# Projections by seven block products, with their results kept in DRAM

## The chip, the cores and the metric

The kernel runs on one core of a Trainium2 chip. The metric is the device time of one execution in microseconds. TensorE multiplies matrices, VectorE and ScalarE do element-wise work, GpSimd (POOL) and SyncE (SP) issue DMA transfers here; the engines run side by side and wait for each other by semaphores.

## The reference

One layer of a decoder trunk on 1024 tokens of 1024 channels, in float32:

```python
h = rms_norm(x, norm_w) * (1.0 + scale) + shift          # shift, scale, gate = silu(c) @ ada_w + ada_b
hq, hf, hi, hz, gq, gk, gv, gz, ga, mg = split(h @ w_in)  # 9232 columns
y_h = hgrn2_branch(hq, hf, hi, hz, ...)   # 8 heads: gated linear recurrence, norm over all, times silu(hz)
y_g = gla_branch(gq, gk, gv, gz, ga, ...) # 4 heads, value width 256, norm per head, times silu(gz)
merged = sigmoid(mg[0]) * (y_h @ w_branch[0]) + sigmoid(mg[1]) * (y_g @ w_branch[1])
out = rms_norm(x + gate * (merged @ w_out), final_norm_w)
```

Both branches are `chunked_gated_linear_attention`: within a chunk all pairs of steps with their decay, between chunks a state of keys by values.

## The kernel before

Every dense product is made of three float32r products: each operand is split into hi + lo (`split`, L150 to L159: a ScalarE copy, L155, and a VectorE subtraction, L158), and hi·hi, hi·lo and lo·hi are summed in PSUM. A `Feat` job makes one tile of 128 features by 1024 tokens: for each of eight k tiles 3 x 2 matmuls of 128x512 (L414). A `Vblk` job makes 256 features of v with tokens on the partitions (L473 to L475, 256 columns a matmul). The jobs run in one list: GLA's projections, the gates of branch 1, branch 1 (`w_branch[0, 1]`), HGRN's projections, the gates of branch 0, branch 0, and the output projection (`OutBlk`, L1078 to L1080). The first six feature tiles are made earlier, k by k, while the modulation is loaded (L309, and L332 for the second half of the tokens).

`Stream.go` runs the jobs; one unit is a k step of six matmuls. `weave` runs a step of the attention when the units that its last `yield` asked for have passed. `ahead` loads weights two jobs ahead and splits them one ahead, if buffers are free. All data stays in SBUF, in 46 buffers of 4 KB per partition (`Slots`); buffers are handed out in program order, first freed first. Only the gated product of branch 1 passes through DRAM (`t1_dram`).

The attention of a head (`attention`, L487 to L663): products of q and decays on VectorE (L504 to L507), small TensorE products of 32 steps (L511, L543, L572, L579, L585) whose results are masked into `blk` and `scT`, scalings of q and k in between (L513 to L549, L591, L592), then transposes of k (L621), state updates (L640, L646) and outputs (L657, L659), which `post` squares and multiplies with the gate.

The order of instructions on each engine comes from a planner that may move ready work ahead of older work; at the start (L124 to L284) the order is that of the program. The engines themselves run their queues in order.

Of the kernel before, what the change touches and what calls it, by code (L numbers as in the profile page):

```python
# [25 lines left out]
N_SLOTS = 46  # L26
ROOM = 9
LOOK = 6


class Slots:
    """Buffers of 4 KB per partition, handed out and given back in program order."""

    def __init__(self, pool, n):
        self.pool = pool
        self.free_list = deque(range(n))
        self.owner = {}
        self.serial = 0

    def get(self, shape, dtype=F32):  # L40
        i = self.free_list.popleft()
        self.serial += 1
        t = self.pool.tile([P] + list(shape), dtype, tag=f"s{i}", name=f"b{self.serial}")
        self.owner[id(t)] = (i, t)
        return t

    def free(self, *tiles):
        for t in tiles:
            self.free_list.append(self.owner.pop(id(t))[0])


@with_exitstack
def hybrid_trunk_kernel(
# [11 lines left out]
    sp = ctx.enter_context(tc.tile_pool(name="slots", bufs=1))  # L65
    dp = ctx.enter_context(tc.tile_pool(name="dram", bufs=1, space=bass.MemoryType.DRAM))
    ps_d = ctx.enter_context(tc.tile_pool(name="ps_d", bufs=2, space=bass.MemoryType.PSUM))
    ps_s = ctx.enter_context(tc.tile_pool(name="ps_s", bufs=1, space=bass.MemoryType.PSUM))
    ps_m = ctx.enter_context(tc.tile_pool(name="ps_m", bufs=2, space=bass.MemoryType.PSUM))
    S = Slots(sp, N_SLOTS)  # L70
    cnt = [0]

    def dtile():
        cnt[0] += 1
        return ps_d.tile([P, T], F32, tag="d", name=f"pd{cnt[0]}")
# [5 lines left out]
    sc_ps = ps_s.tile([P, T], F32, name="sc_ps")  # L81

    # ---------------------------------------------------------------- constants
# [5 lines left out]
    nc.gpsimd.memset(eps_t, EPS)  # L89
    one_t = ones[:, 0:1]  # L90
# [5 lines left out]
    rows_c = cp.tile([8, P], F32, name="rows_c")  # L96
    rows_a = cp.tile([24, P], F32, name="rows_a")
    rows_b = cp.tile([22, P], F32, name="rows_b")
# [5 lines left out]
    def load_x(t):  # L104
        b = S.get([D])
        nc.sync.dma_start(b, x2[t * P:(t + 1) * P, :])
        return b

    row_load(nc.sync, rows_c, c[0])
    x_t = [load_x(t) for t in range(4)]  # L110
# [5 lines left out]
    row_load(nc.gpsimd, rows_b[20:22, :], gla_norm_w[0])  # L116

    def vec_rows(rows, n, at):
        pv = mtile()
        i = nc.tensor.transpose(pv[:, 0:n], rows, ident[0:n, 0:n])  # L120
        nc.vector.tensor_copy(vec[:, at:at + n], pv[:, 0:n])
        return i

    order = ExitStack()  # L124
    order.enter_context(tc.manual_schedule(engines={
        mybir.EngineType.PE, mybir.EngineType.Activation, mybir.EngineType.DVE}))
# [3 lines left out]
    warm = cp.tile([P, 1], F32, name="warm")  # L130
    nc.scalar.activation(warm, cs[:, 0:1], AF.Sqrt)
    nc.vector.tensor_mul(cs, cs, vec[:, R_C:R_C + 8])

    # ---- buffers of the attention, which the start borrows
    scT = cp.tile([P, NCH, P], F32, name="scT")
    blk = cp.tile([P, NCH, 32], F32, name="blk")
    xb = cp.tile([P, 32, 80], F32, name="xb")
    scT_f = scT.rearrange("p c t -> p (c t)")
    xb_f = xb.rearrange("p b c -> p (b c)")

    # ---------------------------------------------------------------- x: norm and transpose, modulation
    h_hi = [S.get([T], F32R) for _ in range(KT)]
    h_lo = [S.get([T], F32R) for _ in range(KT)]
    hT = {}
# [5 lines left out]
    def split(src, hi=None, lo=None, eng=None, pin=False):  # L150
        """src (fp32) = hi + lo with both parts float32r."""
        if hi is None:
            hi = S.get(list(src.shape[1:]), F32R)
            lo = S.get(list(src.shape[1:]), F32R)
        i = nc.scalar.copy(hi, src)  # L155
        if pin:
            tc.keep_in_program_order(i)
        (eng or nc.vector).tensor_sub(lo, src, hi.bitcast(F32))  # L158
        return hi, lo  # L159

    def norm_x(half, xs):
        for i, xt in enumerate(xs):
            t = half * 4 + i
            acc, r = ssx[:, t:t + 1], rsx[:, t:t + 1]
            junk = S.get([D])
            nc.scalar.activation(junk, xt, AF.Square, accum_out=acc)
            S.free(junk)
# [4 lines left out]
    def transpose_x(half, xs, d):  # L172
        if d % 2 == 0:
            hT[half, d // 2] = S.get([2, 512])
        pt = mtile()
        for i in range(4):
            nc.tensor.transpose(pt[:, i * P:(i + 1) * P], xs[i][:, d * P:(d + 1) * P], ident)
        dst = hT[half, d // 2][:, d % 2, :]
        nc.scalar.copy(dst, pt)
        if d == KT - 1:  # L180
            S.free(*xs)

    def make_h(half, d):
        b = hT[half, d // 2][:, d % 2, :]
        sl = slice(half * 512, half * 512 + 512)
        nc.scalar.activation(b, b, AF.Identity, bias=modv[:, 0, d:d + 1], scale=amul[:, d:d + 1])
        split(b, h_hi[d][:, sl], h_lo[d][:, sl])

    def load_mod(d0, nd):
        kq = 4 // nd  # L190
        parts = []
        for kk in range(KT // kq):
            b = S.get([kq, 2, nd * P])
            for half in range(2):
                c0 = half * D + d0 * P
                nc.sync.dma_start(b[:, :, half, :], ada_w[0, kk * kq * P:(kk + 1) * kq * P, c0:c0 + nd * P].rearrange(
                    "(k p) f -> p k f", p=P))
            parts.append(b)
        return parts

    def make_mod(d0, nd, parts, on_pe):
        kq = 4 // nd
        acc = scT_f[:, (d0 // 2 % 2) * 512:(d0 // 2 % 2) * 512 + 2 * nd * P].rearrange("p (a f) -> p a f", a=2)
        for k in range(on_pe, KT):
            src = parts[k // kq][:, k % kq]
            if k == on_pe:
                i = nc.vector.tensor_scalar_mul(acc, src, cs[:, k:k + 1])
                if on_pe:
                    tc.keep_in_program_order(i)
            else:  # L210
                nc.vector.scalar_tensor_tensor(acc, src, cs[:, k:k + 1], acc, ALU.mult, ALU.add)
        pm = mtile()
        for half in range(2):
            for i in range(nd):
                o = pm[:, half * nd + i:half * nd + i + 1]
                for k in range(on_pe):
                    nc.tensor.matmul(o, parts[k // kq][:, k % kq, half, i * P:(i + 1) * P], cs[:, k:k + 1],
                                     start=(k == 0), stop=False)
                nc.tensor.matmul(o, acc[:, half, i * P:(i + 1) * P], one_t, start=(on_pe == 0), stop=True)
        S.free(*parts)  # L220
        nc.vector.tensor_add(modv[:, :, d0:d0 + nd], pm[:, 0:2 * nd].rearrange("p (a b) -> p a b", a=2),
                             vec[:, R_SH:R_SH + 16].rearrange("p (a b) -> p a b", a=2)[:, :, d0:d0 + nd])
        nc.vector.scalar_tensor_tensor(amul[:, d0:d0 + nd], modv[:, 1, d0:d0 + nd], 1.0,
# [9 lines left out]
    def wg(part, k, f):  # L233
        wa, wb = ((wa_hi, wb_hi), (wa_lo, wb_lo))[part]
        if f < 4:
            return wa[k // 2][:, k % 2, f * P:(f + 1) * P]
# [898 lines left out]
```

## Time and profile before

| | |
|---|---|
| runs | 1284.68, 1285.58, 1287.28 us; median 1285.58 |
| profiled execution | span 1287.7 us |
| TensorE busy | 1254.3 us, 97% |
| VectorE busy | 659.9 us, 51% |
| ScalarE busy | 408.8 us, 32% |
| GpSimd busy | 89.1 us, 7% |
| DMA | 86.00 MB, mean 67 GB/s |

In a row of the profile, `L414 PE MATMUL pd<-b,b 128*128 128x512 f32 x3168 | 750.1, 393` reads: line 414, TensorE, operation, output and inputs by the program's names, stationary operand, moving shape, count, then busy microseconds together and mean nanoseconds of one. PEld are weight loads, DVE is VectorE, ACT is ScalarE. In a timeline the first two numbers are start and duration in microseconds, and in brackets stands the idle time before and what ended it. In a row of windows come the window, its length, then busy time of each engine with counts, the granted clock of TensorE, the share of the DMA engines and GB/s. A float32 matmul of the attention stands in two records.

### The profile page before, as it was taken

The numbers are of one execution on the slowest core, as the hardware profiler recorded it, in microseconds if no ns is written. First come the engines' busy times: TensorE is split into PE (matmuls) and PEld (weight loads), VectorE is DVE, ScalarE is ACT, GpSimd is POOL, SyncE is SP. The second block draws the span as 40 slices with busy tenths as digits, with TensorE's granted clock in tenths as the row PEclk, the third lists the DMA queues.
The fourth block names the chain that finished last, engine by engine and source line by source line (L and its number), as shares of the span: only waits on it lengthen the run. The fifth ranks groups of instructions, "written<-read, shape, count | busy, mean of one in ns | idle before, by whom it ended". The sixth has DMA issues, their size and how long they took to land.

```text
span 1287.7 us, 20979 instructions
## 1 busy us (share of the span) xinstructions
PE 1254.3 (97%) x9179; PEld 1059.2 (82%) x9179; DVE 659.9 (51%) x1053; ACT 408.8 (32%) x606; POOL 89.1 (7%) x104
## 2 busy tenths in 40 slices
PE   4899999999999999999999999999999999999997
PEld 3767889889898888888889879888988888878886
DVE  5736334563837362224564556375466430585534
ACT  4566712333223241112232332333233231222222
POOL 5500000000000000000000000000000000140000
PEclk9799999999999999999999999999999999999999
DMA  8613010202002103363010201020010111333302
GB/s 273 224 33 90 26 34 2 66 2 66 18 19 65 34 17 115 122 211 92 18 34 18 82 2 34 17 83 18 18 50 18 50 50 50 131 98 130 132 33 99
DMA packets 99822, 86.00 MB, mean 67 GB/s; under 512 B 3211, under 2 KB 89281, under 8 KB 99730
## 3 DMA queue, kind: packets, MB, share of 16 engines
q1 hardware_dynamic: 98242, 80.24, 20.2%
q0 software_dynamic: 1440, 4.40, 0.9%
q8 instruction: 72, 1.18, 0.4%
q14 instruction: 20, 0.16, 0.0%
q10 hardware_dynamic: 48, 0.01, 0.0%
HBM read 76.25 MB, written 8.39 MB: 66 GB/s over the span
## 4 chain that ended last, share of the span: by engine, by line
PE 61%; DVE 2%; issue 0%; POOL 0%; ACT 0%; POOLq 0%; DVEq 0%; ACTq 0%
PE pd L414 41%; PE pd L473 2%; PE pd L474 2%; PE pd L475 2%; PE pd L1080 2%; PE pd L1079 2%; PE pd L1078 2%; PE pm L657 1%; PE pm L659 1%; PE pm L640 1%; PE sc_ps L511 1%; PE sc_ps L543 1%; PE pm L621 0%; DVE b L158 0%; PE sc_ps L572 0%
## 5 line engine op out<-in xcount | busy, mean ns | idle before, releaser
L414 PE MATMUL pd<-b,b 128*128 128x512 f32 x3168 | 750.1, 393 | 1.7 <-DVE b L1026 1.7
L414 PEld LDWEIGHTS pd<-b,b 128*128 128x128 f32 x3168 | 587.4, 188 | 125.9 <-DVE b L1026 2.1
L158 DVE TENSOR_TENSOR b<-b,b 128x1024 fp32r<-128x1024 f32 (+1 forms) x143 | 171.8, 1216 | 191.9 <-ACT b L155 112.5
L155 ACT CAST b<-b 128x1024 fp32r<-128x1024 f32 (+1 forms) x143 | 134.6, 955 | 302.8 <-PE pd L414 86.3
L473 PE MATMUL pd<-b,b 128*128 128x256 f32 x512 | 149.6, 292 | 0.0
L475 PE MATMUL pd<-b,b 128*128 128x256 f32 x512 | 144.9, 283 | 0.0
L474 PE MATMUL pd<-b,b 128*128 128x256 f32 x512 | 144.8, 283 | 0.0
L473 PEld LDWEIGHTS pd<-b,b 128*128 128x128 f32 x512 | 98.0, 191 | 1.4
L474 PEld LDWEIGHTS pd<-b,b 128*128 128x128 f32 x512 | 98.1, 192 | 0.5
L475 PEld LDWEIGHTS pd<-b,b 128*128 128x128 f32 x512 | 98.0, 191 | 0.0
L591 DVE TENSOR_TENSOR b<-b,tot 128x512 f32<-128x512 f32 x36 | 24.8, 690 | 71.3 <-PE sc_ps L572 27.5
L1078 PE MATMUL pd<-b,b 128*128 128x512 f32 x128 | 49.8, 389 | 0.0
L1079 PE MATMUL pd<-b,b 128*128 128x512 f32 x128 | 49.8, 389 | 0.0
L1080 PE MATMUL pd<-b,b 128*128 128x512 f32 x128 | 49.8, 389 | 0.0
L965 POOL TENSOR_TENSOR b<-b,b 128x1024 f32<-128x1024 f32 x7 | 17.5, 2495 | 464.8 <-ACT b L954 464.8
L758 ACT ACTIVATE b<-pd 128x1024 f32<-128x1024 f32 x24 | 24.6, 1026 | 73.7 <-PE pd L414 73.7
L657 PE MATMUL pm<-scT,b 128*128 128x128 f32 x256 | 46.8, 274 | 0.0
L646 DVE SCALAR_TENSOR_TENSOR b<-b,tot,pm 128x128 f32<-128x128 f32 (+1 forms) x72 | 28.2, 391 | 31.9 <-PE pm L640 30.3
L659 PE MATMUL pm<-b,b 128*128 128x128 f32 x224 | 43.3, 275 | 0.0
L657 PEld LDWEIGHTS pm<-scT,b 128*128 128x128 f32 x256 | 39.2, 191 | 1.7
L855 ACT ACTIVATE b<-pd 128x1024 f32<-128x1024 f32 x16 | 16.4, 1026 | 73.9 <-PE pd L414 73.9
L759 DVE TENSOR_TENSOR b<-b,pd 128x1024 f32<-128x1024 f32 x24 | 29.2, 1218 | 18.8 <-ACT b L758 18.8
(191 smaller groups left out, 1264.2 us busy)
## 6 DMA issues: line engine op xcount, KB each, us to landing
b<-in_w_in_dram SPq DMA_DIRECT2D x66, 512.0 KB, 3.7
b<-in_x_dram SPq DMA_DIRECT2D x16, 512.0 KB, 5.6
b<-in_ada_w_dram SPq DMA_DIRECT2D x32, 256.0 KB, 5.9
b<-in_w_branch_dram SPq DMA_DIRECT2D x16, 512.0 KB, 4.1
t_dram<-b POOLq DMA_DIRECT2D x8, 512.0 KB, 3.6
b<-in_ada_w_dram SPq DMA_DIRECT2D x8, 512.0 KB, 5.4
b<-t_dram SPq DMA_DIRECT2D x8, 512.0 KB, 4.4
b<-in_w_out_dram SPq DMA_DIRECT2D x8, 512.0 KB, 4.6
```

The lines of the kernel that those rows point to most:

```text
L155: i = nc.scalar.copy(hi, src)
L158: (eng or nc.vector).tensor_sub(lo, src, hi.bitcast(F32))
L414: nc.tensor.matmul(ps[0:w, th * 512:(th + 1) * 512], a[:, k, 0:w], b[:, th * 512:(th + 1) * 512], start=(k == 0 and n == 0), stop=(k == KT ...
L473: nc.tensor.matmul(o, lh, hi[:, k % 4, :], start=(k == 0), stop=False)
L474: nc.tensor.matmul(o, lh, lo[:, k % 4, :], start=False, stop=False)
L475: nc.tensor.matmul(o, ll, hi[:, k % 4, :], start=False, stop=(k == KT - 1))
L657: nc.tensor.matmul(o, vch(ch)[:, vh * P:(vh + 1) * P], scT[:, ch, :], start=True, stop=(ch == 0))
L659: nc.tensor.matmul(o, state(ch)[:, vh * P:(vh + 1) * P], q[:, ch * P:(ch + 1) * P], start=False, stop=True)
L759: nc.vector.tensor_mul(s, s, ps)
L1078: nc.tensor.matmul(po, lh, hi[:, k % 2, :], start=(k == 0), stop=False)
L1079: nc.tensor.matmul(po, lh, lo[:, k % 2, :], start=False, stop=False)
L1080: nc.tensor.matmul(po, ll, hi[:, k % 2, :], start=False, stop=(k == KT - 1))
```

## The change

**Products.** All projections but the output projection are made in `Pair` jobs: two tiles of 128 features (rows 1 and 2), 1024 inputs in two halves, 1024 tokens in two halves. The 2x2 blocks are multiplied with seven block products instead of eight, each 128 features by 512 inputs by 512 tokens (12 matmuls of 128x512). `Pair.prep` makes the four sums of weight blocks on VectorE and splits each of the seven operands; `build` makes and splits the seven operands of the activations, once per phase, into tiles of their own (112 KB per partition). The results are combined in three PSUM banks ("a", "b", "e"): products add to a bank, ScalarE copies of a bank (`seed`, `snap`) carry a partial sum to another, and two outputs are summed on VectorE (`add_out`). `Stream` orders the products of neighbouring pairs in turns (`order`), splits up to three products ahead (`LEAD`) and loads when ten small buffers are free.

**Stages.** The input projections are 36 pairs: for GLA four times q with k, two v tiles, two z tiles; for HGRN four times q, f, v, z of two heads, each but the last group followed by a pair of gates of branch 1; then the last such pair and four pairs of gates of branch 0. Their results go to DRAM, as do the alphas, the branch outputs, the gates and t1; stores are issued by GpSimd (`store`), loads by SyncE. v is made in feature layout and turned on TensorE two products later (`late`). Then `drain_side` runs what is left of the attention, `phase(1)` projects GLA's branch, while HGRN's norm (`hgrn_norm`) and the gate of the modulation (`gate_side`) run beside it, and `phase(0)` projects HGRN's. The output projection stays as it was, with other buffers.

**Buffers.** SBUF has 8 buffers of 4 KB (attention, activations), 22 of 2 KB (weights, results); PSUM has a ring of five banks, one for the attention's scores and two for the rest.

**Start.** Products 1, 5 and 2 of the first four pairs run while the modulation of each half of the channels comes in; there is no part with a fixed order. The modulation's sums over k are TensorE products with `csz`.

**Attention.** The q product is no longer part of xb (80 columns become 48) but a product of its own into `pq`; GLA's values are handled in two halves of 128; silu and sigmoid are single ScalarE operations; q's factor is in the epsilon of GLA's norm (`epsk_t`); HGRN's decay and k are made from the fetched f. The yields are 4, 6, 5, 3, 2.5, 2.5 and 2 up to the transposed k, then 1 and four times 2 for each 128 values, after 3 (GLA) or 3 and 3 (HGRN) for the fetch; GLA's norm has four more of 2. The alphas ask 30 units.

The core of the diff (lines of the new kernel with +):

```diff
+N_S = 8
+N_Q = 22
+N_RING = 5
+EARLY = 4
+LEAD = 3
+LOADS = 6
...
+    sc_ps = ps_s.tile([P, 512], F32, name="sc_ps")
...
+        for kk in range(2):
+            if p == 1:
+                hsplit(1, kk, Y["11"][kk])
+            elif p == 5:
+                sub(Y["11"][kk], Y["12"][kk], Y["11"][kk])
+                hsplit(5, kk, Y["11"][kk])
+            elif p == 6:
+                sub(Y["11"][kk], Y["22"][kk], Y["11"][kk])
...
+                sub(Y["12"][kk], Y["12"][kk], Y["22"][kk])
+                hsplit(7, kk, Y["12"][kk])
...
+        def load(self, *names):
+            for n in names:
+                f, kh = int(n[0]) - 1, int(n[1]) - 1
+                self.x[n] = Q.get()
+                nc.sync.dma_start(self.x[n].rearrange("p (k f) -> p k f", k=4),
+                                  self.src[f][kh * 512:(kh + 1) * 512, :].rearrange("(k p) f -> p k f", p=P))
...
+        def split(self, p, t):
+            hi = Q.get(dtype=F32R)
+            nc.scalar.copy(hi, t)
+            lo = Q.get(dtype=F32R)
+            nc.vector.tensor_sub(lo, t, hi.bitcast(F32))
+            Q.free(t)
+            self.w[p] = (hi, lo)
...
+        def prep(self, p):
+            x, add = self.x, nc.vector.tensor_add
+            if p == 1:
+                if "21" in x:
+                    x["s3"] = Q.get()
+                    add(x["s3"], x["11"], x["21"])
+                self.split(1, x.pop("11"))
...
+                self.split(p, x.pop({2: "12", 7: "s3", 3: "s4", 4: "22"}[p]))
...
+        def matmuls(self, p, kt, bank, start):
+            hi, lo = self.w[p]
+            h_hi, h_lo = H[p]
+            sl = slice(kt * P, (kt + 1) * P)
+            for n, (a, b) in enumerate(((hi, h_hi), (hi, h_lo), (lo, h_hi))):
+                nc.tensor.matmul(bank, a[:, sl], b[:, kt, :], start=(start and kt == 0 and n == 0),
+                                 stop=(kt == 3 and n == 2), skip_group_check=True)
...
+            elif p == 2:
+                a = bank.pop("a")
+                self.out(0, 0, a, False)
+                R.free(a)
+            elif p == 7:
+                self.add_out(1, 1, bank["b"], self.snap[5], ALU.add)
...
+            elif p == 4:
+                b = bank.pop("b")
...
+    BANK = {1: "a", 2: "a", 5: "e", 3: "e", 6: "b", 7: "b", 4: "b"}
...
+        def f(i, half, ap, summed):
+            t = ap if summed else Q.get()
+            if func is not None:
+                nc.scalar.activation(t, ap, func)
+            elif not summed:
+                nc.scalar.copy(t, ap)
+            store(names[i], half, t)
+            Q.free(t)
+        return f
...
+            def turn():
+                pt = mtile()
+                for j in range(4):
+                    nc.tensor.transpose(pt[:, j * P:(j + 1) * P], t[:, j * P:(j + 1) * P], ident)
+                u = Q.get()
+                nc.scalar.copy(u, pt)
+                Q.free(t)
+                store(names[i], half, u)
+                Q.free(u)
+            late.append([2, turn])
...
+            for i in range(n):
+                order += [(i, 6), (i + 1, 1), (i, 2), (i, 7), (i + 1, 5), (i, 3), (i, 4)]
+            self.order = [z for z in first + order if z[0] < n]
...
+            while self.prepped < len(self.seq):
+                i, p = self.seq[self.prepped]
+                must = self.prepped <= s
+                if not must and (self.prepped > s + LEAD or Q.room() < 6):
+                    break
+                if i not in self.loaded:
+                    if not must and Q.room() < 10:
+                        break
+                    self.load(i)
+                self.jobs[i].prep(p)
+                self.prepped += 1
+            for z in self.seq[self.prepped:self.prepped + LOADS]:
+                if z[0] not in self.loaded and Q.room() >= 10:
+                    self.load(z[0])
...
+                for kt in range(4):
+                    job.matmuls(p, kt, job.bank[key], start)
+                    if kt % 2:
+                        weave(1)
+                job.after(p)
...
+        pq = mtile()
         for b in range(32):
             ch, j = b // 4, b % 4
+            nc.tensor.matmul(pq[32 * j:32 * j + 32, ch * 32:ch * 32 + 32], k[:, b * 32:b * 32 + 32],
+                             q[:, b * 32:b * 32 + 32], start=True, stop=True)
...
+    def fetch(src, shape=None):
+        t = S.get(shape)
+        nc.sync.dma_start(t, src.rearrange("p (a b) -> p a b", b=shape[1]) if shape else src)
+        return t
...
+    def hgrn_attention(h):
+        q, f = fetch(h_q[h]), fetch(h_f[h])
+        k = S.get()
+        yield 3
+        nc.scalar.activation(k, f, AF.Sigmoid, scale=-1.0)
+        nc.scalar.activation(f, f, AF.Sigmoid)
...
+        yield from attention(q, k, f, [(get_v, post)])
+        nc.gpsimd.dma_start(y_h[h], y[0])
+        if h == 0:
+            nc.gpsimd.dma_start(ssq_d, sq[0])
+        else:
+            nc.gpsimd.dma_start(ssq_d, sq[0], accum_op=ALU.add)
...
+        for h in range(8):
+            y = fetch(y_h[h])
+            yield 2
+            nc.vector.tensor_mul(y, y, rst)
+            nc.gpsimd.dma_start(y_h[h], y)
...
+        def then(h=h):
+            start_side(gla_attention(h), 4)
+        add(col(C_GZ + 2 * h * P), col(C_GZ + (2 * h + 1) * P), evac(g_z[2 * h:2 * h + 2], AF.Silu), then)
...
+        add(*both(C_HQ), evac(h_q[h:h + 2], AF.Silu))
+        add(*both(C_HF), evac(h_f[h:h + 2], None))
+        add(*both(C_HI), evac_v(h_v[h:h + 2]))
+        def then(h=h):
+            start_side(hgrn_attention(h), 4)
+            start_side(hgrn_attention(h + 1), 1)
+        add(*both(C_HZ), evac(h_z[h:h + 2], AF.Silu), then)
+        if h < 6:
+            mg_pair(1, mg1, h)
+    mg_pair(1, mg1, 6)
+    for i in range(0, 8, 2):
+        mg_pair(0, mg0, i)
...
+    start_side(alpha_side(), 2)
+    w_stream.run()
+    drain_side()
...
+    def fetch_y(src):
+        for kh in range(2):
+            for half in range(2):
+                n = f"{kh + 1}{half + 1}"
+                y_get(n)
...
+            g = Q.get()
+            nc.sync.dma_start(g, gates[d][:, sl])
+            nc.vector.tensor_mul(g, g, ap)
...
+    def phase(branch, src, gates, put):
+        fetch_y(src)
+        for p in PRODUCTS:
+            build(p)
+        js = [Pair(w_branch[0, branch, :, d * P:(d + 1) * P], w_branch[0, branch, :, (d + 4) * P:(d + 5) * P],
+                   gated(d, d + 4, gates, put)) for d in range(4)]
+        Stream(js).run()
+    start_side(hgrn_norm(), 16)
+    start_side(gate_side(), 1)
+    phase(1, y_g, mg1, put_t1)
+    drain_side()
+    phase(0, y_h, mg0, put_m)
```

1298 lines of the change are left out of this document (616 added, 682 removed).

## The prediction

> **What bounds the kernel now.** I read the totals and groups of the page first, then the timeline for the pace, then the rows of the stages that the change adds to.
>
> ```profile
> span 1287.7 us, 20979 instructions
> PE 1254.3 (97%) x9179; PEld 1059.2 (82%) x9179; DVE 659.9 (51%) x1053; ACT 408.8 (32%) x606; POOL 89.1 (7%) x104
> ...
> L414 PE MATMUL pd<-b,b 128*128 128x512 f32 x3168 | 750.1, 393 | 1.7 <-DVE b L1026 1.7
> L473 PE MATMUL pd<-b,b 128*128 128x256 f32 x512 | 149.6, 292 | 0.0
> ```
>
> TensorE is busy 97% of the span and VectorE 51%. L414 is the feature-layout projection (66 jobs of 48 matmuls), L473 to L475 the token-layout one for v, 512 records each. A duration of 393 ns overlaps its neighbour, so the pace has to come from the timeline. In the output projection VectorE takes each finished block of 24 matmuls at once, waiting for TensorE each time:
>
> ```profile
> 1214.60 0.69 DVE L1083 TENSOR_TENSOR xb<-pd,b 128x512 f32<-128x512 f32 x1 [2.49 <-PE pd L1080]
> ...
> 1225.48 0.69 DVE L1083 TENSOR_TENSOR xb<-pd,b 128x512 f32<-128x512 f32 x1 [2.49 <-PE pd L1080]
> ```
>
> Two blocks in 10.88 us give 10.88 / 48 = 0.2267 us per 512-column matmul. For v:
>
> ```profile
> 302.42 0.28 PE L475 MATMUL pd<-b,b 128*128 128x256 f32 x1
> ...
> 303.49 0.28 PE L475 MATMUL pd<-b,b 128*128 128x256 f32 x1
> ```
>
> These are ten starts in a row, nine intervals: 0.119 us per 256-column matmul.
>
> ```profile
> L414 PE MATMUL pd<-b,b x3168: 387/389/793, 120.8 to 1192.4; 128*128 128x512 f32 x198
> ```
>
> Before 120.8 us the kernel had done the 288 matmuls of the first six tiles, 65.3 us of work at that pace; the start is therefore 55.5 us behind a kernel that is dense from time zero. Dense work is 3168 + 288 + 384 matmuls of 512 columns (870.5 us) and 1536 of 256 (182.8 us), 1053.3 us together; what is left of the span is the attention's and the start.
>
> So TensorE sets the end and any matmul saved counts, if it stays fed. Where the attention's instructions stand in its order decides what follows.
>
> ```profile
> 990.46 0.63 DVE L504 TENSOR_TENSOR xb<-b,b 128x256 f32<-128x256 f32 x1
> ...
> 990.99 0.68 DVE L591 TENSOR_TENSOR b<-b,tot 128x512 f32<-128x512 f32 x1
> ...
> L511 PE MATMUL sc_ps<-xb,b x768: 232/233/257, 180.5 to 1015.4; 128*32 128x80 f32 x192
> ...
> L543 PE MATMUL sc_ps<-xb,b x768: 206/206/230, 188.8 to 1023.2; 128*32 128x48 f32 x192
> ```
>
> On VectorE the planner lets ready work go ahead of older work: L504 of head 7 runs before the last L591 of head 6. On TensorE, never short of ready dense work, the attention keeps its program place: the last head's L511 and L543 are five units of dense work apart in the program (5 x 6 x 0.2267 = 6.8 us) and 7.8 us apart in the trace.
>
> **The change, part by part.** The terms are made against the profiled span of 1287.7 us; the median of the runs is 2.1 us less.
>
> *1. Dense matmuls.* 36 input pairs and 8 branch pairs, 7 products each, 4 x 3 matmuls a product: 44 x 84 = 3696, and 384 unchanged in the output projection, 4080. Before, 3840 and 768 (v's, counted as 512 columns), 4608. 528 x 0.2267 = 119.7 us go. The v blocks also change pace, 182.8 us becoming 768 x 0.2267 = 174.1. Together **-128.4**.
>
> *2. TensorE work added.*
>
> ```profile
> L657 PE MATMUL pm<-scT,b 128*128 128x128 f32 x256 | 46.8, 274 | 0.0
> L659 PE MATMUL pm<-b,b 128*128 128x128 f32 x224 | 43.3, 275 | 0.0
> ...
> L511 PE MATMUL sc_ps<-xb,b 128*32 128x80 f32 x768 | 15.8, 234 | 0.0
> ...
> L640 PE MATMUL pm<-b,b 128*128 128x128 f32 x112 | 15.0, 274 | 0.0
> ...
> L621 PE MATMUL pm<-ident,b 128*128 128x128 f32 x84 | 11.1, 272 | 0.0
> ...
> L543 PE MATMUL sc_ps<-xb,b 128*32 128x48 f32 x768 | 10.7, 208 | 0.0
> ...
> L572 PE MATMUL sc_ps<-b,b 128*32 128x16 f32 x768 | 8.8, 185 | 0.0
> ...
> L585 PE MATMUL sc_ps<-b,b 128*64 128x64 f32 x192 | 8.2, 228 | 0.0
> ...
> L579 PE MATMUL sc_ps<-b,b 128*32 128x32 f32 x384 | 5.5, 199 | 0.0
> ```
>
> 16 v tiles are made in feature layout and turned: 16 x 2 x 4 = 128 transposes of L621's kind, 128 x 11.1 / 84 = 16.9 us. The q product leaves xb and gets its own 32 small matmuls a head, 768 records as wide as L579's: 768 x 5.5 / 384 = 11.0. L511 falls from 80 columns to L543's 48: -5.1. **+22.8**, with no cover, since TensorE is the bound.
>
> *3. Attention left over at the end of the input stream.* A unit is six dense matmuls. The stream has 36 x 14 - 24 = 480 (12 products of the first four pairs are done before it). The side asks 30 units for the alphas, 4 x 54 for GLA, 8 x 40 for HGRN, and 38 in its start waits: 604. So 124 are left when the input projections end, three whole HGRN heads (5, 6, 7), and these are drained with nothing dense beside them. The branch phase can't fill in: its fetch takes all eight 4 KB buffers, which the heads hold. Before, 64 units of gate jobs stood behind the last head.
>
> What a head costs alone, from the rows of one:
>
> ```profile
> 955.29 0.64 DVE L504 TENSOR_TENSOR xb<-b,b 128x256 f32<-128x256 f32 x1
> ...
> 960.54 0.61 DVE L529 TENSOR_TENSOR tot<-b 128x256 f32<-128x256 f32 x1
> ...
> 1015.88 0.42 DVE L518 TENSOR_TENSOR blk<-sc_ps,eye 128x256 f32<-128x256 f32 x1
> ...
> 1021.25 0.60 DVE L595 TENSOR_TENSOR tot<-tot 128x32 f32<-128x32 f32 x3
> 1023.50 0.96 DVE L548 TENSOR_TENSOR b<-b,tot 128x768 f32<-128x768 f32 x1 [1.66 <-PE sc_ps L543]
> ...
> 1025.74 0.20 DVE L559 COPY_PREDICATED blk<-mask,sc_ps 128x32 f32<-128x32 int32 x1
> ...
> L591 DVE TENSOR_TENSOR b<-b,tot 128x512 f32<-128x512 f32 x36 | 24.8, 690 | 71.3 <-PE sc_ps L572 27.5 <-PE sc_ps L579 26.7 <-PE sc_ps L585 17.1
> ...
> L646 DVE SCALAR_TENSOR_TENSOR b<-b,tot,pm 128x128 f32<-128x128 f32 x48 | 16.7, 347 | 8.3 <-PE pm L640 7.1
> ...
> L1086 ACT ACTIVATE xb<-b 128x512 f32<-128x512 f32 x16 | 10.1, 634 | 57.7 <-DVE b L1084 35.3 <-issue 22.4
> ...
> L935 ACT ACTIVATE b<-pd 128x1024 f32<-128x1024 f32 x8 | 8.2, 1028 | 13.9 <-PE pd L414 13.9
> ...
> b<-in_w_in_dram SPq DMA_DIRECT2D x66, 512.0 KB, 3.7
> ...
> t_dram<-b POOLq DMA_DIRECT2D x8, 512.0 KB, 3.6
> ...
> b<-t_dram SPq DMA_DIRECT2D x8, 512.0 KB, 4.4
> ```
>
> One period, from fetch to fetch (the next head's f waits for the buffer of k): fetch 4.4; four ACT passes of 1.03, 4.1; VectorE's front and first scalings 5.9; its second stretch 1015.88 to 1021.85 less one foreign L158 of 1.2 inside, 4.8; third stretch 2.4; three times L591 with its twin L592, 4.1; TensorE's small matmuls, each step once on the path, (10.7 + 11.0 + 10.7 + 8.8 + 5.5 + 8.2) / 12 = 4.6; two ACT copies into X 1.0 and seven transposes 0.9; the clamp, L598 and the turns between engines are taken as 3. Sum 35 us. Head 5's fetch, sigmoids and front, some 12 us, can be done before the stream ends; the last head has 8 more after its transposes (seven L646 2.4, L657 and L659 5.6 for 30 records of 90.1 / 480). From the stream's end to the last attention matmul: 35 - 12 + 35 + 35 + 8 = 101 us. TensorE's own part, already in the 1287.7, is 4.6 + 0.9 + 1.9 (L640) + 5.6 = 13 a head, 39. **+62**; bounds 18 (only one head left over: 31 - 13) and 85 (a period of 43).
>
> During this TensorE is mostly idle, and the clock may answer.
>
> ```profile
> 0.00:20.00 20.00, 6.97 (x30) 6.05 (x30) 5.99 (x15) 9.14 (x17) 13.41 (x55) 1.00 0.93 280
> 20.00:40.00 20.00, 13.61 (x47) 10.70 (x46) 16.24 (x27) 7.52 (x15) 6.79 (x6) 0.85 0.75 243
> ```
>
> In the start TensorE was busy 68% of 20 us at a clock of 0.85, and 35% at 1.00: no clear price, so none is in the sum. The Trainium skill (TensorE: Matmul & The Clock Gate, section "HAM oscillation — how this bites in real kernels") says that an idle gap of more than about 3.4 us puts the clock back to half. The rows bear it out only in part: a fall is there, not to a half, and not in the idler window. By that rule the sum would be 26 us more (rival D).
>
> *4. Start of the first branch phase.* Y12 lies in the buffer of head 7's v, free after its last matmul: fetch 4.4, then a subtraction, a copy and a subtraction of 128x1024.
>
> ```profile
> 1059.77 1.23 DVE L158 TENSOR_TENSOR b<-b,b 128x1024 fp32r<-128x1024 f32 x1 [0.57 <-ACT b L155]
> ...
> 1172.36 1.29 DVE L1027 TENSOR_TENSOR b<-b,b 128x512 f32<-128x512 f32 x2
> ```
>
> That is 4.4 + 1.23 + 1.05 + 1.23 = 8 us to product 5. Then VectorE has the builds of products 5, 6, 2, 7, 3, 4, 20 operations of 1.23 = 24.6, and two to three of 0.65 (L1027) of weights for each of the eight products, some 10: done 39 us after the fetch began, against 8 x 12 x 0.2267 = 21.8 us of matmuls. **+20** taken with two product-1 blocks done early; 8 to 25.
>
> *5. Start of the second phase.* Builds 1 and 5 can go ahead as soon as the last pair has used these tiles, 8 to 10 products before the end of the phase, so VectorE's work is covered; DMA may not be. In the phase's 76 us move weights, gates, t1, HGRN's y read and written, the gate's matrix and the next Y, seven times 4.2 MB = 29 MB.
>
> ```profile
> 560.00:570.00 10.00, 10.00 (x45) 8.26 (x45) 1.00 0.68 214
> ```
>
> 214 GB/s took 0.68 of the engines, so they hold some 315: 29 MB are 93 us. Worst case +19, best 0: **+10**.
>
> *6. Gaps inside the input stream.* VectorE per pair: four additions, seven splits, two sums, 13 x 0.65 = 8.5 us; a head's 25 us (17.2 of the path above, the states 2.4, the rest for the clamp, masks and results) in 40 units adds 0.62 a unit, 8.7 for 14. Per pair TensorE takes 19.0 + 14 x 0.33 (13 / 40) + the transposes, 24: VectorE stands at 72%. It fits, but with 22 small buffers the next weights wait for old ones: the block x21 of pair i+2 goes into the slot of output (1,1) of pair i, which is sum 0.65, activation 0.63 (L1086), store 3.6, load 3.7, then addition, copy, subtraction 1.9: 10.5 us, more where the activation table has to change; in that time TensorE has four products, 10.9, and eight units of attention, 2.6. Two to three microseconds are over. A head has two VectorE stretches longer than that (6.6 and 4.5 us in some 69), met by one pair in six, each overshooting by about 4: 6 x 4 = **+24**. Bounds 0 (attention's steps fill the gaps) and 119 (3.3 us at every pair: the slack gone and as much again, from slower stores).
>
> *7. The opening.* x of half the tokens, half of ada_w, weights, the other half: 15.7 MB at the 262 GB/s of the two windows above, 60 us; then modulation, builds and two rounds of products until about 97 us, by which 192 matmuls (43.5 us) are done: 54 behind, as before. **0**, -15 to +15.
>
> The branch phases and the output projection change nothing else on the path: gates and t1 are fetched a product ahead, and the last pair's m is needed last (k order 0, 4, 1, 5 ...).
>
> Sum: 1287.7 - 128.4 + 22.8 + 62 + 20 + 10 + 24 = 1298.1 us profiled, **1296** as a median: the saved matmuls are spent on a drain that has no dense work left.
>
> **The rivals.**
>
> A (forecast): as summed; its own range 1275 to 1318.
>
> B, faster, 1234: the attention runs ahead. Whenever the stream has a gap TensorE takes attention steps from further down, so that only one head is left when it ends. It decides from the point where 80 units or more are gained. Then term 3 is 18, term 6 is 0: 1298.1 - 44 - 24 = 1230, and with a little left of the gaps 1236; less 2.1, 1234. For it: VectorE's order above, and every period of a head alone (35 us) is shorter than its 40 units (54 us dense). Against it: TensorE kept the program order in all of the trace, and a kernel with no gaps never gets ahead.
>
> C, much slower, 1350: the recycling of small buffers binds at each pair. Term 6 is 119, of which some 40 come back as attention done in the gaps: 1298.1 + 95 - 40 = 1353. For it: the slack of two to three microseconds rests on a store landing in 3.6 us, measured where little else moved, and now every pair moves 2 MB and every head 3. Against: that is 2.1 + 14 / 40 x 3.1 = 3.2 MB in 24 us, 132 GB/s of some 315.
>
> D, slower, 1322: the drain throttles the clock, as the start did at 0.85. If TensorE's 39 us there take twice as long and two thirds of them lie on the chain, +26; at 0.85 it would be 5. The Trainium skill's rule is the one named above.
>
> E, the change doesn't do what it says: the pace of a matmul worsens because each of a pair's products changes its weights every matmul. The totals show as many weight loads as matmuls already (9179 of each), so I give it nothing.
>
> **How the numbers follow.** A 0.42, B 0.33, C 0.18, D 0.07. Within 0.2% of the old median (1283.0 to 1288.2, about what a measurement can tell) only A has a share, one in seven; below it another one in six. Faster: 0.33 + 0.07 = 0.40; same 0.06; slower 0.54. The range runs from B's good half to C's middle, 1226 to 1356; A alone is 1275 to 1318.
>
> **What would show it.** Right: a stretch of some 100 us before the first branch product in which TensorE is under half busy, L-lines of three HGRN heads in it, VectorE waiting for TensorE and the reverse; a second, shorter hole after it; dense matmuls at 0.227 us; 4080 of them. Term 6 wrong: waits of the weight loads on stores, spread evenly over the stream. B right: no hole before the branch phase, TensorE over 95% throughout. The forecast falls if TensorE's busy share stays where it was.

## The result and the profile after

The changed kernel takes 1351.28 us (median of 4 runs, 1349.09 to 1356.57) against 1285.57 us: a ratio of 1.051, 95% interval 1.0486 to 1.0533. It is slower, as forecast, but by 66 us where 10 were forecast. The profiled execution spans 1354.9 us, 56.8 more than the sum of 1298.1; it is the slowest of the four runs, so a stretch of it can be several microseconds longer than in another.

The totals and the dense group of the page, and the waits of TensorE (waiting line, what it waited for, total us, times, longest):

```profile
span 1354.9 us, 22696 instructions
PE 1193.3 (88%) x8883; PEld 951.9 (70%) x8883; DVE 893.8 (66%) x1552; ACT 640.2 (47%) x1075; POOL 126.1 (9%) x259
...
L299 PE MATMUL rb<-h,qb 128*128 128x512 f32 x3672 | 910.1, 403 | 74.7 <-ACT qb L260 28.2
```
```profile
PE rb L299 <- ACT qb L260: 28.2, 7, 8.9
PE rb L299 <- DVE qb L262: 19.4, 5, 13.2
```

TensorE fell from 97% to 88% busy, VectorE rose from 660 to 894 us, and the transfers from 86 to 200 MB. The dense waits are few and long, 28.2 us in seven places and 19.4 in five, so they sit somewhere in particular. The windows by stage (stretch, its length, busy time of PE, PEld, DVE, ACT and POOL with instruction counts, granted clock, DMA share, GB/s) say where: input stream, drain of the attention, branch phases, output projection.

```profile
100.00:934.00 834.00, 810.57 (x6408) 661.37 (x6408) 556.30 (x1032) 432.69 (x735) 88.79 (x161) 0.99 0.43 135
934.00:1034.00 100.00, 48.43 (x1082) 41.60 (x1081) 64.42 (x150) 32.95 (x64) 4.45 (x6) 0.68 0.37 109
1034.00:1258.00 224.00, 173.87 (x674) 133.36 (x673) 168.32 (x209) 80.53 (x115) 14.33 (x26) 0.87 0.67 217
1258.00:1355.00 97.00, 87.48 (x383) 71.28 (x381) 49.71 (x85) 29.55 (x64) 0.00 (x0) 0.97 0.25 90
```

Set against the forecast, from its last stage backward (output 95.3 us as before; phases 672 x 0.2267 + 20 + 10 = 182; drain 101; so the stream's end at 920); the stages of the trace end at 934.6, 1033.6 and 1257.6 us:

| stage | forecast | trace | difference |
|---|---|---|---|
| start and input stream | 920 | 934.6 | +15 |
| drain of three HGRN heads | 101 | 99 | -2 |
| two branch phases | 182 | 223.9 | +42 |
| output projection | 95 | 97.3 | +2 |

In the profiles of four experiments below that leave the stream as it is (the builds, the norm, both with idle matmuls) its end lies at 925 to 930 us, so 5 to 10 of the 15 us are common to all of them.

The drain is there as drawn. Its steps on TensorE in the timeline (start, length, tiles, count, wait before it and its releaser) for head 6, and the start of head 7:

```profile
966.89 0.76 PE L670 MATMUL pm<-sb,sb 128*32 128x32 f32 x64
972.77 1.51 PE L674 MATMUL sc_ps<-xb,sb 128*32 128x48 f32 x64 [5.11 <-DVE xb L665]
978.32 1.51 PE L704 MATMUL sc_ps<-xb,sb 128*32 128x48 f32 x64 [4.04 <-DVE xb L700]
982.22 1.05 PE L733 MATMUL sc_ps<-sb,sb 128*32 128x16 f32 x64 [2.39 <-DVE blk L715]
984.89 0.65 PE L740 MATMUL sc_ps<-sb,sb 128*32 128x32 f32 x32 [1.62 <-DVE blk L759]
987.64 1.12 PE L746 MATMUL sc_ps<-sb,sb 128*64 128x64 f32 x16 [2.09 <-ACT scT L767]
990.25 1.73 PE L782 MATMUL pm<-ident,sb 128*128 128x128 f32 x7 [1.49 <-DVE sb L753]
...
999.17 0.76 PE L670 MATMUL pm<-sb,sb 128*32 128x32 f32 x64
```

A period of 999.17 - 966.89 = 32.3 us, forecast as 35: nearly every step waits for VectorE or ScalarE, and nothing dense stands between.

Most of the surplus is in the phases, clearest at the seam between them (the last matmul of the first phase ends at 1151.3 us, the second runs freely from 1179.3). Windows of all engines there, then the last of VectorE's builds of the new Y, and the wait of TensorE that they end:

```profile
1150.00:1160.00 10.00, 1.26 (x6) 0.72 (x4) 7.50 (x9) 6.31 (x7) 1.08 (x2) 0.73 1.06 380
1160.00:1170.00 10.00, 2.44 (x4) 1.00 (x4) 8.92 (x8) 5.17 (x7) 0.00 (x0) 0.50 0.52 133
1170.00:1180.00 10.00, 0.66 (x2) 0.56 (x3) 10.00 (x12) 2.25 (x4) 0.00 (x0) 0.50 0.00 0
```
```profile
1166.65 2.35 DVE L223 TENSOR_TENSOR sb<-sb,sb 128x1024 f32<-128x1024 f32 x2
...
1173.46 2.35 DVE L228 TENSOR_TENSOR sb<-sb,sb 128x1024 f32<-128x1024 f32 x2
1175.73 0.68 DVE L271 TENSOR_TENSOR qb<-qb,qb 128x512 f32<-128x512 f32 x1
1176.33 2.35 DVE L205 TENSOR_TENSOR h<-sb,h 128x1024 fp32r<-128x1024 f32 x2
1178.60 0.68 DVE L262 TENSOR_TENSOR qb<-qb,qb 128x512 fp32r<-128x512 f32 x1
```
```profile
1179.34 15.84 PE L299 MATMUL rb<-h,qb 128*128 128x512 f32 x56 [13.21 <-DVE qb L262]
```

Thirty microseconds with 4.4 us of TensorE work. First the transfers are full (share 1.06, 380 GB/s: the new Y and, behind it in SyncE's queue, the first weights), then VectorE is (10.00 of 10): it makes all builds one after the other, and the 0.68 us weight operation that TensorE waits for stands behind them. After it the phase runs without a gap.

### The profile page after: what moved, and what is told of

Read it like the earlier page. It is cut to its first block, busy times and chain, and to the rows that moved or that the text cites. A ratio compares the mean times of both kernels' runs of the same rounds, so it can differ in the third digit from the quotient of the medians.

```text
span 1354.9 us, 22696 instructions
## 1 busy us (share of the span) xinstructions
PE 1193.3 (88%) x8883; PEld 951.9 (70%) x8883; DVE 893.8 (66%) x1552; ACT 640.2 (47%) x1075; POOL 126.1 (9%) x259
## 4 chain that ended last, share of the span: by engine, by line
issue 67%; PE 14%; POOL 7%; DMA 6%; DVE 4%; ACT 2%; SPq 0%; POOLq 0%; DVEq 0%; ACTq 0%
PE rb L299 6%; PE rb L1173 2%; PE rb L1174 2%; PE rb L1172 2%; DMA ssq<-sb 1%; POOL mg L416 1%; DMA hy<-sb 1%; DVE h L205 1%; DMA qb<-in_w_in_dram 1%; POOL hz L416 1%; POOL gz L416 1%; POOL gv L416 1%; POOL hv L416 1%; DMA sb<-hy 1%; POOL hf L416 1%
## 5 line engine op out<-in xcount | busy, mean ns | idle before, releaser
L299 PE MATMUL rb<-h,qb 128*128 128x512 f32 x3672 | 910.1, 403 | 74.7 <-ACT qb L260 28.2
L299 PEld LDWEIGHTS rb<-h,qb 128*128 128x128 f32 x3672 | 689.9, 192 | 243.8 <-ACT qb L260 31.2
L260 ACT CAST qb<-qb 128x512 fp32r<-128x512 f32 x308 | 185.1, 619 | 226.5 <-PE rb L299 68.4
L262 DVE TENSOR_TENSOR qb<-qb,qb 128x512 fp32r<-128x512 f32 x308 | 208.1, 686 | 100.3 <-ACT qb L260 81.7
L271 DVE TENSOR_TENSOR qb<-qb,qb 128x512 f32<-128x512 f32 x40 | 27.5, 688 | 88.8 <-DMA qb<-in_w_in_dram 62.3
L810 PE MATMUL pm<-scT,sb 128*128 128x128 f32 x256 | 47.4, 277 | 3.2 <-DVE sb L800 2.3
L205 DVE TENSOR_TENSOR h<-sb,h 128x1024 fp32r<-128x1024 f32 x36 | 43.2, 1220 | 10.0 <-ACT h L204 10.0
L810 PEld LDWEIGHTS pm<-scT,sb 128*128 128x128 f32 x256 | 39.4, 192 | 6.6 <-DVE sb L800 3.4
L812 PE MATMUL pm<-sb,sb 128*128 128x128 f32 x224 | 43.3, 275 | 0.0
L312 DVE TENSOR_TENSOR qb<-rb,qb 128x512 f32<-128x512 f32 x44 | 30.2, 686 | 15.5 <-PE rb L299 15.1
L286 DVE TENSOR_TENSOR qb<-qb,qb 128x512 f32<-128x512 f32 x44 | 30.2, 687 | 10.4 <-PE rb L299 9.2
L284 DVE TENSOR_TENSOR qb<-qb,qb 128x512 f32<-128x512 f32 x44 | 30.3, 688 | 8.8 <-DMA qb<-in_w_in_dram 5.0
L793 PEld LDWEIGHTS pm<-sb,sb 128*128 128x128 f32 x224 | 32.5, 211 | 3.3 <-ACT sb L783 1.3
L812 PEld LDWEIGHTS pm<-sb,sb 128*128 128x128 f32 x224 | 34.0, 192 | 0.0
L312 DVE TENSOR_TENSOR qb<-qb,rb 128x512 f32<-128x512 f32 x44 | 29.9, 680 | 5.5 <-PE rb L299 5.4
```

The lines of the kernel that those rows point to most:

```text
L205: nc.vector.tensor_sub(lo, src, hi.bitcast(F32))
L260: nc.scalar.copy(hi, t)
L262: nc.vector.tensor_sub(lo, t, hi.bitcast(F32))
L284: add(x["s2"], x["s3"], x["22"])
L299: nc.tensor.matmul(bank, a[:, sl], b[:, kt, :], start=(start and kt == 0 and n == 0), stop=(kt == 3 and n == 2), skip_group_check=True)
L312: nc.vector.tensor_tensor(t, in0, in1, op)
```

## The experiments

All are edits of the changed kernel, and differences are against its 1351.28 us. Ratios are against the kernel before as it ran beside each experiment (medians of 1286.29 to 1287.47 us, where it had 1285.57); the changed kernel was not run again beside them, so a difference of 2 us means nothing. Theory: the loss is the drain plus, in the phases, VectorE's builds and the norm's round trip. Rivals: small buffers bind (C), the clock binds in the drain (D), or the saved matmuls were not worth their time.

**The attention asks for less cover.** Its steps' `yield`s are shortened so that all heads end within the stream:

```diff
-        yield 6
+        yield 4
...
-        yield 5
+        yield 3.5
```

> The attention's yields of the changed kernel are shortened (4, 6, 5, 3, 2.5, 2.5, 2 become 3, 4, 3.5, 2.5, 2, 2, 1.5; the 2s after them 1.5; the fetches 2; the alphas 2), so that the last HGRN head ends within the 480 units of the input stream; nothing else. Theory 'drain' (the changed kernel's 99 us between the last input matmul at 934 us and the last attention matmul at 1034 us hold only about 39 us of TensorE work): the hole goes, about 1351 - 60 = 1291 us. Rival 'chain too tight' (VectorE, at 68% in the stream, can't deliver a head in 30 units, so TensorE waits in the stream instead): the stream grows by as much as the hole shrinks, 1330 us or more, with waits of TensorE's small products on VectorE inside the stream.

Measured 1310.83 us, 40 less (1.0179 of before, 1.0152 to 1.0206), between the two expectations. The drain is gone; the stream pays with waits that the cover had hidden:

```profile
PE sc_ps L704 <- DVE xb L700: 17.1, 9, 3.4
```

So 40 of the 52 us that TensorE stood idle in the drain's window came back by the medians; these 17 us of waits more than make up the rest.

**Builds behind the first weights.** Each build of Y is issued just ahead of the product that uses it, after earlier products' weight splits:

```diff
+                if p in self.pending:
+                    self.pending.discard(p)
+                    build(p)
...
-        for p in PRODUCTS:
-            build(p)
```

> In the two branch phases each build of a product's activations is put behind the first weight split that needs it, instead of all seven builds ahead of every weight; the operations are the same. Theory 'builds first' (VectorE makes the activations of products 2, 7, 3 and 4 while TensorE waits for one weight block of product 5; 13.2 us of one wait in the second phase): the hole at 1151 to 1180 us falls to about 10 us and the first phase's start loses some 10 us more, together 25 to 35 us, about 1321 us. Rival 'transfers' (the phases wait for DMA, whatever VectorE's order is): 0 to 8 us less, 1343 to 1351 us.

Measured 1332.51 us, 19 less (1.0353, 1.033 to 1.0376): the order on VectorE, with the same operations, costs 19 us. The hole at the seam, 28 us with four matmuls in it, is down to one wait of 10.8 us, as the theory had it; the total falls short of its 25 us:

```profile
1149.05 1.22 PE L299 MATMUL rb<-h,qb 128*128 128x512 f32 x2 [10.80 <-ACT qb L260]
```

The phases take 207 us in this profile (1026.2 to 1233.0) where they took 224.

**The HGRN norm without its round trip.** The norm factor is multiplied into the gates of branch 0 in place of fetching, scaling and storing eight y tiles:

```diff
-        for h in range(8):
-            y = fetch(y_h[h])
-            yield 2
-            nc.vector.tensor_mul(y, y, rst)
-            nc.gpsimd.dma_start(y_h[h], y)
...
+            if rst is not None:
+                nc.vector.tensor_mul(g, g, rst[:, sl])
```

> HGRN's norm factor is multiplied into the gates of branch 0 (16 multiplications of 128x512) instead of fetching, scaling and storing the eight y_h tiles during the first branch phase: 8.4 MB of transfers less, and SyncE's queue no longer stands behind buffers that wait for those stores. Theory 'transfers' (holes of the first phase at 1098 to 1106 and 1120 to 1140 us, and the late Y of the second): first phase some 15 us shorter, second phase's fetch earlier by 10, about 1326 us. Theory 'builds first': the second hole stays near 25 to 30 us since VectorE still makes all builds ahead of the weights, and the total falls by 5 to 10 us, about 1343 us.

Measured 1331.06 us, 20 less (1.0347, 1.0319 to 1.0374), nearer to the first expectation. In its profile the drain ends at 1025.3 us and the output projection begins at 1230.6, 205 us where it had been 224, at 0.60 of the transfers in place of 0.67:

```profile
1025.00:1231.00 206.00, 171.85 (x680) 131.67 (x679) 167.61 (x217) 79.79 (x115) 10.03 (x18) 0.92 0.60 193
```

The hole at the seam shrinks to one wait of 11.6 us, with VectorE's builds still in front of the weights; the 25 to 30 us that the second expectation left there are not seen:

```profile
1148.13 17.12 PE L299 MATMUL rb<-h,qb 128*128 128x512 f32 x64 [11.64 <-DVE qb L262]
```

In the changed kernel SyncE's queue had stood behind these stores: the loads for the gate of the modulation (L936) waited for buffers that the stores of y had to release.

```profile
SPq L936 <- DMA hy<-sb: 15.2, 6, 5.0
```

The fetch of the new Y, behind them in the queue, was issued from 1134 to 1152 us; without the round trip from 1069 to 1106. The edit takes away bytes, buffers and waits of the queue together, and no run separates them.

**All three together.**

> The three edits together. If drain, builds and transfers are the three places where the saved matmuls went, their gains add up: 1351 - 60 - 25 - 15 = about 1250 us, less than the kernel before the change (1285.6). If one of them only moves the wait elsewhere (the stream or the small buffers become the bound), more than 1285.

Measured 1288.52 us (1.0007 of before, 0.9989 to 1.0026): 63 less, where the single gains add up to 79, so they overlap in part: builds and norm both shorten the one hole at the seam. The 1250 us of the first expectation did not come out. From the stream's last activation at 995 us to the first output matmul at 1184 lie some 190 us, where the phases took 224. Most of that stretch:

```profile
1000.00:1184.00 184.00, 164.93 (x665) 127.48 (x666) 163.24 (x215) 77.61 (x113) 8.63 (x16) 0.96 0.63 206
```

VectorE is now busy 163 of 184 us and TensorE 165, so both are near the length of the stretch. Which of them sets it is open; no run took VectorE work alone away.

**An eighth product.** The fourth product's matmuls are issued twice, 528 more, into the same bank (not one of their own, as the expectation says):

```diff
+                if p == 4:
+                    for kt in range(4):
+                        job.matmuls(p, kt, job.bank[key], False)
```

> The changed kernel with one more block product for each pair of feature tiles: the fourth product's 12 matmuls are issued a second time into a buffer of their own, 528 more 128x512 matmuls in all, with nothing else added (the values are then not the reference's). If TensorE's pace sets nearly the whole span, the time rises by what the prediction's first term took off, 528 x 0.2267 = +120 us, to about 1471 us. If other engines and the transfers set much of the time, part of it is hidden: about half or less, 1385 to 1415 us.

Measured 1439.57 us, 88 more: between the two expectations, 0.167 us a matmul where the pace is 0.2267. The stream's last dense matmuls, of the changed kernel and of this one:

```profile
929.69 4.92 PE L299 MATMUL rb<-h,qb 128*128 128x512 f32 x21
```
```profile
1003.77 4.01 PE L299 MATMUL rb<-h,qb 128*128 128x512 f32 x17
```

The two profiled runs are 84 us apart. 73 of these came in the stream, for 432 matmuls or 98 us of work; the span from there to the output projection grew by 11, for 96 matmuls or 22 us. So about a quarter of the work vanishes in the stream (a sixth, if the stream's end is taken at the 927 us of the four other profiles) and half of it in the phases. That matmuls saved there are worth as much less is concluded from matmuls added, not measured.

**Three small buffers fewer.** `N_Q` 22 becomes 19.

> The changed kernel with 19 small 2 KB buffers in the rotation in place of 22. If the recycling of these buffers holds up every pair (the prediction's rival at 1350), three fewer make it clearly slower: 1375 us or more. If it does not, the time stays within 10 us of the changed kernel's, 1341 to 1361 us.

Measured 1359.61 us, 8 more (1.0552, 1.0535 to 1.057), as the second expectation has it. Rival C falls as the main cause: a rotation that bound at every pair would not lose three buffers for 8 us. More than 22 were not tried.

**Idle matmuls in the drain.** They keep TensorE at work between the attention's steps:

```diff
-            for _ in side.popleft()[0]:
-                pass
+            for units in side.popleft()[0]:
+                if warm:
+                    for _ in range(int(2 * units)):
+                        nc.tensor.matmul(bank, H[1][0][:, 0, 0:P], H[1][0][:, 1, :], start=True, stop=True,
+                                         skip_group_check=True)
```

> The changed kernel with some 245 idle matmuls put between the steps of the attention that is left over after the input stream (two 128x512 matmuls for each unit a step asks for, into a bank nobody reads), so that TensorE has work in its waits. If the half clock of that stretch lies on its chain, as the prediction's rival D has it, the clock stays near 1.00, the stretch falls from 99 us to about 84 to 88, the first branch products start at full clock, and the time falls by 12 to 20 us, to 1331 to 1339 us. If the chain runs over VectorE and the transfers and TensorE's slower steps are hidden, the clock rises and the time stays within 6 us of 1351.

Measured 1354.45 us (1.0529, 1.0508 to 1.055): no gain, though the clock in the drain rose from 0.68 to 0.95:

```profile
934.00:1034.00 100.00, 87.91 (x1226) 70.86 (x1214) 65.24 (x149) 31.29 (x61) 4.75 (x6) 0.95 0.35 102
```

> The same with half as many idle matmuls (one for each unit, some 125 in all), because with two the fill itself held up steps: between the two wide score steps of a head it stood for 4.84 us where 3.90 us lay between their starts before. If the half clock costs time on the chain, the thinner fill shows it: a head's period of 32.3 us falls to 28 to 30 us, and the time by 6 to 12 us, to 1339 to 1345 us. If the chain runs over VectorE and the transfers, the period stays at 31.5 us or more and the time within 4 us of 1351.

Measured 1353.28 us (1.0522, 1.0504 to 1.0539). All of its fill had gone by the middle of head 6. From head 6's first step to head 7's, the first half at full clock:

```profile
962.62 0.76 PE L676 MATMUL pm<-sb,sb 128*32 128x32 f32 x64
...
994.30 0.76 PE L676 MATMUL pm<-sb,sb 128*32 128x32 f32 x64
```

That is 31.7 us against 32.3 at half clock. The drain as a whole took 99.5 us with two idle matmuls a unit (930.0 to 1029.5) and 103.3 with one (925.5 to 1028.9), against 99.0 without (934.6 to 1033.6), and the phases behind it took 224 to 225 us in all three. Where the fill stood it also delayed two steps of a head by up to 2 us, so a price of a few microseconds can't be excluded; the 26 us of rival D can.

**All three repairs, and gates moved.** Three pairs of gates of branch 1 move from between the HGRN groups (not from behind the stream, as the expectation can be read) behind the last group, and the step ahead of L704's products gets one more unit of cover:

```diff
-        yield 6
+        yield 5
...
-        if h < 6:
-            mg_pair(1, mg1, h)
-    mg_pair(1, mg1, 6)
+    for i in range(0, 8, 2):
+        mg_pair(1, mg1, i)
```

> The kernel with all three repairs together, and in addition 15 groups of dense work (the gates of the second branch that need only loaded weights) moved from behind the projections' stream into its end, with one attention step given more dense work to cover it, so that the last attention head still ends before the stream does. If the attention's steps and waits are what the dense work cannot fill, the moved work fills holes and the time falls by about 15 us, to 1270 to 1278 us, faster than before the change. If VectorE sets the pace in the stream by now, the moved work brings nothing: 1284 to 1292 us.

Measured 1274.11 us: 0.9897 of before, 0.9882 to 0.9911, within the first expectation. The wait that the further unit covers shrank, from the version with the three repairs (first row) to this one:

```profile
PE sc_ps L708 <- DVE xb L704: 19.2, 10, 4.1
```
```profile
PE sc_ps L708 <- DVE xb L704: 4.4, 3, 2.5
```

(The line numbers are those of these versions: L708 is L704 of the changed kernel.) How much of the 14 us is the unit and how much the move wasn't tried apart. TensorE's 92% in its page is still 5 points under the kernel before:

```profile
PE 1175.5 (92%) x8883; PEld 938.5 (74%) x8883; DVE 890.7 (70%) x1560; ACT 627.7 (49%) x1068; POOL 121.3 (10%) x251
```

## Why the prediction was right in sign and wrong in size

**Terms 1 and 2, matmuls saved and added.** The count (3672 + 24 + 384 = 4080) and the pace hold: a run of 24 in the first phase gives (5.60 - 0.39) / 23 = 0.2265 us.

```profile
1094.70 5.60 PE L299 MATMUL rb<-h,qb 128*128 128x512 f32 x24
```

The transposes, by the groups of TensorE with their shapes, took 19.4 us where 16.9 were forecast:

```profile
L442 PE MATMUL pm<-ident,qb 128*128 128x128 f32 x128 | 19.4, 274 | 4.0 <-DVE qb L312 4.0
```

What did not hold is the condition in the premise above them, that "any matmul saved counts, if it stays fed": the eighth product shows 88 us for the 528, not 119.7. The missing 32 us are best read not as a further term but as the holes of terms 4 to 7 seen from the other side; that is an argument, not a measurement.

**Term 3, the drain.** Right: 99 us against 101, a period of 32.3 against 35, heads 5 to 7. Taking it away returned 40 us against the forecast's +62; steps that stood in the drain then wait inside the stream (17.1 us at L704 alone).

**Terms 4 and 5, the starts of the phases: the step that failed.** Forecast 20 + 10 = 30 us with upper bounds of 25 and 19 (for the second its own 93 and 76 us give 17); the phases took 224 us for 152 us of matmuls, 72 over, and TensorE stood idle for 50 of these. Term 5 said that "VectorE's work is covered" since builds 1 and 5 can go ahead, and left only transfers open. The trace has it the other way at the end: Y came late, and then all the builds stood in front of the weights. Two omissions made it. One is VectorE's work and its order: it was costed per pair in the stream (72%) and never summed for the phases, where two rounds of builds, the norm, the gates and the weights make 168 us. That sum alone would be 16 us more than the matmuls; what the runs priced is the order, 19 us for the builds in front of the weights. The other is that the norm's y was booked as bytes (29 MB with the rest), not as a chain: its stores hold buffers, loads in SyncE's queue wait for these, and the fetch of the new Y stands behind them. Dropping the round trip gave 20 us. With all repairs the phases came down by some 34 us, most of the 42 by which the two terms fell short; the rest is open. The clock, 0.87 on average there, lengthens what runs beside the holes; how much of the 72 us that is wasn't isolated.

**Terms 6 and 7, gaps and opening.** Between 100 and 934 us TensorE was idle for 834 - 810.6 = 23 us, 24 forecast, but that the two agree is partly luck. Some 7 of the 23 us lie before 140 us and belong to the opening, and in the rest the dense line waits most not for weights, as drawn, but for the sum of two outputs (L312). In the longest of these waits, 3.7 us, that sum stood on VectorE behind an addition of weights (L271) that had waited 5.6 us for its load; in the next, 2.9 us, behind a stretch of a head.

```profile
PE rb L299 <- DVE qb L312: 9.2, 5, 3.7
```
```profile
DVE qb L271 <- DMA qb<-in_w_in_dram: 62.3, 22, 6.9
```

So loads came late, as term 6 had it, in 22 places, and TensorE had work for most of that time. The 15 us by which the stream ended late were lost ahead of it. Forecast were 192 dense matmuls by 97 us; the windows of the dense line (busy time, count) have 195 by 120, and the timeline shows a wait for a weight split there, and then 12 matmuls in twice their time:

```profile
0.00:120.00 120.00, 52.36 (x195) 0.91 0.54 173
```
```profile
100.57 5.79 PE L299 MATMUL rb<-h,qb 128*128 128x512 f32 x12 [6.96 <-ACT qb L260]
```

So the opening was some 20 us late where the term had 0 with a bound of 15, and about 5 were made up later (10 to 15 in the four other profiles). Here too the trace shows operations that the sum had not put in order, builds and weight splits on two engines. No run changed the opening alone.

**Rivals.** B: no; TensorE didn't take attention steps ahead, and three heads were left. C: its time of 1350 is what came out, but not its mechanism. The stream's gaps are 23 us and not 119, three buffers fewer cost 8 us, and the small stores, taken at 3.6 us, landed in 2.8:

```profile
mg<-qb POOLq DMA_DIRECT2D x32, 256.0 KB, 2.8
```

E: no; the pace held. D: the clock did fall (window of TensorE alone):

```profile
940.00:950.00 10.00, 1.72 (x80) 0.50 0.46 163
```

By the rule of the Trainium skill (TensorE: Matmul & The Clock Gate, section "HAM oscillation — how this bites in real kernels") an idle gap of more than about 3.4 us puts the clock back to half. Here the trace agrees, with 0.50 in a window that holds a wait of 8.7 us, where the opening of the kernel before had shown 0.85. Its price did not follow: the drain was no longer than the sum without it, and filling it brought nothing.

## What to carry to other kernels

Saving work on the bound engine moves the bound: sum every other engine's work again for each stage that shrinks, not only for the longest one; here VectorE's 168 us in the branch phases exceeded the 152 us of matmuls left, and the order of that work counted for as much as its sum. Where an order is written by hand, cover that was sized for more dense work has to be sized again, and long preparatory work belongs behind the short operation that the bound engine waits for first. A total that matches a rival's number says nothing until its waits are found where that rival puts them.

## What the runs showed of the hardware

The 64 small matmuls of L704 took 1.51 us in the drain at about half clock (above), and 0.89 with the clock held at 1.00 by the idle matmuls (L710 there): 1.7 times, not twice.

```profile
1010.72 0.89 PE L710 MATMUL sc_ps<-xb,sb 128*32 128x48 f32 x64 [2.08 <-DVE xb L706]
```

As each step waits for VectorE or ScalarE, the time of the kernel didn't follow. The transfers reached 380 GB/s in one window of ten microseconds, above the 315 that the forecast took from 214 GB/s at a share of 0.68. And a 512 KB store landed in 6.3 us (y of HGRN, the median of 16) where that of another tensor, t1, had landed in 3.6 in the kernel before:

```profile
hy<-sb POOLq DMA_DIRECT2D x16, 512.0 KB, 6.3
```
